# Staggered SBUF places for the operands of the matrix products

## The chip, the core and the metric

The kernel runs on one core of a Trainium2 chip. The metric is device time in microseconds of one execution. Two runs of the kernel before took 2041.06 and 2042.29 us, median 2041.67.

## What is computed

Two transformer blocks, one after the other, on a sequence of 512 tokens of width 1024, in float32. Cut to the products, which are nearly all of the work:

```python
# first block
x = x + 0.5 * swiglu(rmsnorm(x, ffn1_norm), ffn1_wgu, ffn1_wdown)   # d_ff 2816
z = rmsnorm(x, mix_norm) @ w_in                                      # q, k, v, conv, gates
a = sliding_window_attention(q, k, v, sinks) @ attn_proj
c = silu(layernorm(causal_depthwise_conv(u, dw_w, dw_b))) @ conv_proj
x = x + (sigmoid(ga) * a + sigmoid(gb) * c) @ w_out
x = x + 0.5 * swiglu(rmsnorm(x, ffn2_norm), ffn2_wgu, ffn2_wdown)
x = x + sigmoid(rmsnorm(x, ple_gate_norm) @ ple_gate_w) * rmsnorm(p @ ple_proj, ple_norm)
# second block
h = h + concat(pool_mixer(...), deltanet_mixer(...)) @ w_out_2       # from rmsnorm(h) @ w_in_2
h = h + memory_cross_attention(rmsnorm(h), rmsnorm(mem), w_xq, w_xk, w_xv, w_xo)
h = h + relu(rmsnorm(h) @ w_up) ** 2 @ w_down                        # d_ff 4096
return rmsnorm(h, final_norm_g)
```

## The kernel before

Activations lie transposed: a tile of 128 partitions, eight chunks (one for each 128 of the 1024 channels) and 512 tokens in a chunk. Weights come as *units*: one unit is the block of 128 output channels over all input channels, a tile of 128 x 1024 (eight parts of 128 columns; fewer in some units). `unit_plan` lists all 357 of them in the order of use.

Each product is made in three steps to keep float32 accuracy. A float32 operand is split into a high part, written as float32r by the scalar engine (a rounding copy), and a low part, the difference, written by the vector engine. `w_split` does this for a unit's weights: the staged tile `wst` becomes `wh` (L188, ACT) and `wl` (L189, DVE). `split` does it for activations (`xh` and `xl`, `hh` and `hl`, and others). `mm3` then issues, for one part k, three matmuls into the same PSUM tile: wh x xh (L227), wh x xl (L228), wl x xh (L229). The weights' 128 columns are the stationary operand, loaded anew by TensorE for every matmul; the 512 (or 256) tokens of an activation chunk are the moving operand. A unit is eight such triples, and then its PSUM tile is evacuated.

The order on PE is the program's; a scheduler places the other engines' work. Weight transfers run four units ahead (`AHEAD_DMA`), splits two (`AHEAD_SPLIT`); `wst` has two buffers, `wh` and `wl` three each.

Places in SBUF, as the built program has them (byte offsets in a partition). The eight-chunk tiles all come from `big`: five buffers of 16,384 bytes at 27328 + 16384 n, chunk k at 2048 k in them. `wh` has its three buffers at 135872 + 4096 n, `wl` at 148160 + 4096 n, part k at 512 k in them. Each of these starts 704 bytes past a multiple of 2048. In the cross attention of the second block, the products of `xhead` (L1360) read the stationary operand from `xv` (at 176832, again 704 past a multiple of 2048, its pieces at multiples of 512) and the moving one from `pth` and `ptl` (201536 and 205632, both 832 past a multiple of 2048).

In `dn_blocks` (the delta rule's 16 x 16 triangular blocks) a vector operation multiplies into a small temporary of 16 x 15 with a buffer of its own, tag `t16`; another temporary there, `g16`, is 16 x 16.

Of the kernel before, what the change touches and what calls it, by code (L numbers as in the profile page):

```python
# [9 lines left out]
F32 = mybir.dt.float32  # L10
F32R = mybir.dt.float32r
# [4 lines left out]
P = 128  # L16
S = 512
D = 1024
ND = D // P
# [87 lines left out]
class Kern:  # L107
# [18 lines left out]
        return f"{s}_{self.n}"  # L126

    def big(self, s, dt=F32):
        return self.pb.tile([P, 8, S], dt, tag="b16", name=self.nm(s), bufs=5)

    def c5(self, s, bufs=10):
        return self.pm.tile([P, 542], F32, tag="c5", name=self.nm(s), bufs=bufs)
# [43 lines left out]
    def w_split(self, i, parts=1):  # L176
        if i >= len(self.plan) or i in self.split_:
            return
        self.w_dma(i)
        nb = self.plan[i][2]  # L180
        st = self.staged[i]
        h = self.pw.tile([P, nb * P], F32R, tag="wh", name=self.nm("wh"), bufs=3)
        l = self.pw.tile([P, nb * P], F32R, tag="wl", name=self.nm("wl"), bufs=3)
        self.split_[i] = (h, l)
        n = nb * P // parts
        for p in range(parts):
            c = slice(p * n, p * n + n)
            r = self.nc.scalar.copy(h[:, c], st[:, c])  # L188
            self.nc.vector.tensor_tensor(out=l[:, c], in0=st[:, c], in1=h[:, c].bitcast(F32), op=ALU.subtract)  # L189
        return r  # L190
# [774 lines left out]
    def dn_blocks(self):  # L965

        nc = self.nc
        v = nc.vector.tensor_tensor  # L970
        u16 = self.pm.tile([P, 16, 16], F32, tag="u16", name="u16")
        ex = lambda t: t.rearrange("p (a c) -> p a c", c=1).to_broadcast([P, 16, 16])
        d16 = self.lcol("d16").rearrange("p (a c) -> p a c", a=1).to_broadcast([P, 16, 16])
        nc.gpsimd.tensor_copy(u16[:], d16)
        sel = []
        for q in range(4):
            sel.append(self.pm.tile([P, 4, P], F32R, tag="A1", name=self.nm("sel"), bufs=4))
            nc.gpsimd.tensor_tensor(
                out=sel[q][:], in0=self.lcol("bd16").rearrange("p (a c) -> p a c", a=1).to_broadcast([P, 4, P]),
                in1=self.bc(self.lcol("d16")[:, 4 * q:4 * q + 4], 4), op=ALU.mult)  # L980
        while self.fronts < 4:
            yield
        g16 = self.pm.tile([P, 16, 16], F32, tag="g16", name="g16")
        v(out=g16[:], in0=ex(self.g_br[:]), in1=d16, op=ALU.mult)
        yield
        ps = self.pd()
        nc.tensor.matmul(ps[:, :256], self.lcol("bd16"), g16[:].rearrange("p a c -> p (a c)"), start=True, stop=True)
        v(out=g16[:], in0=ps[:, :256].rearrange("p (a c) -> p a c", c=16), in1=self.ld[:], op=ALU.mult)
        self.split(self.ldh[:], self.ldl[:], g16[:])
        yield  # L990
        for js in ((0, 1), (2, 3), (4, 5, 6), (7, 8, 9, 10, 11), (12, 13, 14)):
            ps, o = self.pd(), 0
            reps = []
            for j in js:
                w = 16 - j - j % 2
                r = ps[:, o:o + 16 * w].rearrange("p (a c) -> p a c", c=w)
                sj = sel[j // 4][:, j % 4, :]
                nc.tensor.matmul(r, sj, self.ldh[:, :, 16 - w:], start=True, stop=False)
                nc.tensor.matmul(r, sj, self.ldl[:, :, 16 - w:], start=False, stop=True)
                reps.append((j, 15 - j, r[:, :, w - 15 + j:]))  # L1000
                o += 16 * w
            for j, w, r in reps:
                t = self.pm.tile([P, 16, 15], F32, tag="t16", name=self.nm("t16"))
                v(out=t[:, :, :w], in0=r, in1=u16[:, :, j:j + 1].to_broadcast([P, 16, w]), op=ALU.mult)
                v(out=u16[:, :, j + 1:], in0=u16[:, :, j + 1:], in1=t[:, :, :w], op=ALU.add)
            if js[0] == 4:
                yield
        self.u16 = u16
# [637 lines left out]
```

## Time and profile before

| | |
|---|---|
| runs, median | 2041.67 us (2041.06 to 2042.29) |
| the profiled execution | 2041.87 us, span 2040.1 us |
| PE busy | 97% of the span, 9324 matmuls |
| DVE, ACT, POOL busy | 59%, 43%, 13% |
| TensorE clock granted, mean | 0.990 of full speed |
| HBM traffic | 98 GB/s over the span |

The span runs from the first to the last instruction of the profiled execution. Busy time of PE counts overlapping, pipelined matmuls, so it does not tell how fast they follow each other; for that one reads the starts in the timeline. A matmul's record is longer (0.39 us with 512 columns) than the distance to the next start, as matmuls overlap. [...]

### The profile page before, as it was taken

The page shows a single profiled execution, that of the slowest core. Times are in us where ns is not written, and L with a number is a line of the kernel's source. Part 1 is how long each engine was busy: PE and PEld are TensorE (multiplying, and loading weights), DVE is VectorE, ACT ScalarE, POOL GpSimd, SP SyncE. Part 2 cuts the span into 40 slices and gives each one's busy share as a digit, 9 for nine tenths or more (in the row PEclk, how much of TensorE's full clock was granted, in tenths as well). Part 3 has the DMA queues.
Part 4 walks back from the last instruction along what each step waited for, and adds up shares of the span by engine and source line. Part 5 has one row for each costly group of instructions (what it writes and reads, how often), then busy time and mean ns, then how long its engine had stood idle before and what let it go on. Part 6 is the DMA issues. An engine that isn't in the chain of part 4 may idle for free. (4 is left out here: it accounts for less than half of the span.)

```text
span 2040.1 us, 24509 instructions
## 1 busy us (share of the span) xinstructions
PE 1982.6 (97%) x9324; PEld 1649.1 (81%) x9324; DVE 1209.1 (59%) x1909; ACT 875.9 (43%) x1437; POOL 272.7 (13%) x263
## 2 busy tenths in 40 slices
PE   8999999999998999999999999997999999999997
PEld 6888888788787888888888877876989888888886
DVE  6434435799889865543443577666576655344344
ACT  5213223565878543431322364364364444233233
POOL 0000000196224300000000003257000000000001
PEclk9999999999899999999999999998999999999999
DMA  5232233323122134223223234212044422232322
GB/s 182 93 104 93 96 100 103 127 89 101 62 75 65 58 129 158 95 93 100 97 93 103 83 94 136 91 57 83 22 154 131 135 83 93 98 99 93 102 94 73
DMA packets 65669, 200.92 MB, mean 98 GB/s; under 512 B 7312, under 2 KB 11536, under 8 KB 65424
## 3 DMA queue, kind: packets, MB, share of 16 engines
q1 hardware_dynamic: 64864, 198.83, 29.8%
q8 instruction: 74, 1.21, 0.3%
q10 hardware_dynamic: 688, 0.53, 0.1%
q14 instruction: 43, 0.35, 0.1%
HBM read 188.58 MB, written 10.49 MB: 98 GB/s over the span
## 5 line engine op out<-in xcount | busy, mean ns | idle before, releaser
L188 ACT CAST wh<-wst 128x1024 fp32r<-128x1024 f32 (+3 forms) x357 | 353.9, 993 | 894.9 <-PE mm L228 641.0
L227 PE MATMUL mm<-xh,wh 128*128 128x512 f32 x1272 | 502.2, 395 | 2.6 <-ACT xh L291 1.5
L229 PE MATMUL mm<-xh,wl 128*128 128x512 f32 x1272 | 495.7, 390 | 0.7 <-DVE wl L189 0.5
L228 PE MATMUL mm<-xl,wh 128*128 128x512 f32 x1272 | 495.5, 390 | 0.3 <-DVE xl L292 0.3
L189 DVE TENSOR_TENSOR wl<-wst,wh 128x1024 fp32r<-128x1024 f32 (+3 forms) x357 | 421.5, 1182 | 76.8 <-ACT wh L188 76.4
L227 PEld LDWEIGHTS mm<-xh,wh 128*128 128x128 f32 x1272 | 239.0, 188 | 55.1 <-issue 2.7
L228 PEld LDWEIGHTS mm<-xl,wh 128*128 128x128 f32 x1272 | 239.2, 188 | 52.6 <-issue 3.1
L229 PEld LDWEIGHTS mm<-xh,wl 128*128 128x128 f32 x1272 | 239.1, 188 | 51.4 <-DVE wl L189 1.5
L228 PE MATMUL mm<-hl,wh 128*128 128x512 f32 (+1 forms) x616 | 238.2, 387 | 0.2
L227 PE MATMUL mm<-hh,wh 128*128 128x512 f32 (+1 forms) x616 | 238.3, 387 | 0.0
L229 PE MATMUL mm<-hh,wl 128*128 128x512 f32 (+1 forms) x616 | 237.9, 386 | 0.0
L372 DVE SCALAR_TENSOR_TENSOR x<-mm,x 128x512 f32<-128x512 f32 x111 | 76.7, 691 | 249.3 <-PE mm L229 249.3
L652 POOL TENSOR_TENSOR y<-y,cv 128x512 f32<-128x512 f32 x90 | 131.7, 1463 | 126.0 <-ACT cv L651 109.3
L228 PEld LDWEIGHTS mm<-hl,wh 128*128 128x128 f32 x616 | 115.7, 188 | 24.4 <-DVE hl L289 1.0
L227 PEld LDWEIGHTS mm<-hh,wh 128*128 128x128 f32 x616 | 115.7, 188 | 23.5
L229 PEld LDWEIGHTS mm<-hh,wl 128*128 128x128 f32 x616 | 115.7, 188 | 23.2
L227 PE MATMUL mm<-xnh,wh 128*128 128x512 f32 x304 | 120.8, 397 | 0.7 <-DVE z L390 0.7
L228 PE MATMUL mm<-xnl,wh 128*128 128x512 f32 x304 | 119.6, 393 | 0.0
L229 PE MATMUL mm<-xnh,wl 128*128 128x512 f32 x304 | 119.5, 393 | 0.0
L439 DVE TENSOR_TENSOR t<-mm,R 128x512 f32<-128x512 f32 x43 | 29.7, 692 | 138.4 <-PE mm L229 138.3
L660 DVE SCALAR_TENSOR_TENSOR cacc<-u,vec,cacc 128x512 f32<-128x512 f32 x145 | 108.9, 751 | 2.8
L433 DVE TENSOR_TENSOR t<-mm,R 128x512 f32<-128x512 f32 x43 | 29.7, 692 | 94.1 <-PE mm L229 94.0
(421 smaller groups left out, 2800.5 us busy)
## 6 DMA issues: line engine op xcount, KB each, us to landing
wst<-ffn_wgu SPq DMA_DIRECT2D x86, 512.0 KB, 3.4
wst<-w_in SPq DMA_DIRECT2D x63, 512.0 KB, 3.5
wst<-ffn_wdown SPq DMA_DIRECT2D x32, 512.0 KB, 3.5
wst<-w_up SPq DMA_DIRECT2D x32, 512.0 KB, 3.4
wst<-w_down SPq DMA_DIRECT2D x32, 512.0 KB, 3.4
wst<-ffn_wdown SPq DMA_DIRECT2D x16, 384.0 KB, 3.0
xd<-x SPq DMA_DIRECT2D x24, 256.0 KB, 2.3
x<-xd SPq DMA_DIRECT2D x24, 256.0 KB, 5.0
```

Source lines behind the costliest of these rows:

```text
L188: r = self.nc.scalar.copy(h[:, c], st[:, c])
L189: self.nc.vector.tensor_tensor(out=l[:, c], in0=st[:, c], in1=h[:, c].bitcast(F32), op=ALU.subtract)
L227: self.last_mm = mm(ps, h, xh, start=first, stop=False)
L228: mm(ps, h, xl, start=False, stop=False)
L229: mm(ps, l, xh, start=False, stop=last)
L372: self.nc.vector.scalar_tensor_tensor(out=x, in0=ps[:], scalar=scale, in1=x, op0=ALU.mult, op1=ALU.add)
L433: nc.vector.tensor_tensor(out=t[:], in0=ps[:], in1=R[:], op=ALU.mult)
L439: nc.vector.tensor_tensor(out=t[:], in0=ps[:], in1=R[:], op=ALU.mult)
L652: eng.tensor_tensor(out=y, in0=y, in1=t[:], op=ALU.add)
L660: yield eng.scalar_tensor_tensor(out=y if j == 29 else acc, in0=u[:, j:j + S], scalar=w(j), in1=acc, op0=ALU.mult, op1=ALU.add)
```

## The change

Three edits, all on where tiles lie.

- `big` allocates eight chunks of 516 instead of 512 columns and hands out the first 512 of each. So chunk k starts 2064 k bytes into the tile, 16 k bytes further than before, and the five buffers lie 16,512 bytes apart.
- `w_split` always allocates 1036 columns for `wh` and `wl` (1024 and 12 spare ones) and places the unit's parts 4 (i mod 4) columns into the buffer, i being the unit's number in the plan: 0, 16, 32 or 48 bytes. The weight buffers lie 4,160 bytes apart, at 136512 + 4160 n and 148992 + 4160 n.
- The temporary of `dn_blocks` becomes 16 x 16 and shares the tag, hence the buffer, of `g16`, which frees the room that the others take.

Tiles that are allocated behind these move along; `xv` is now at 177856, `pth` at 202560. On every engine's queue the same instructions stand in the same order with the same waits as before; the one row that reads otherwise is a vector multiplication of `dn_blocks` whose output is now 16 x 15 with gaps and was 240 columns in a row.

```diff
     def big(self, s, dt=F32):
-        return self.pb.tile([P, 8, S], dt, tag="b16", name=self.nm(s), bufs=5)
+
+        return self.pb.tile([P, 8, S + 4], dt, tag="b16", name=self.nm(s), bufs=5)[:, :, :S]
...
         st = self.staged[i]
-        h = self.pw.tile([P, nb * P], F32R, tag="wh", name=self.nm("wh"), bufs=3)
-        l = self.pw.tile([P, nb * P], F32R, tag="wl", name=self.nm("wl"), bufs=3)
+        o = 4 * (i % 4)
+        h, l = (self.pw.tile([P, ND * P + 12], F32R, tag=t, name=self.nm(t), bufs=3)[:, o:o + nb * P]
+                for t in ("wh", "wl"))
         self.split_[i] = (h, l)
...
-                t = self.pm.tile([P, 16, 15], F32, tag="t16", name=self.nm("t16"))
+                t = self.pm.tile([P, 16, 16], F32, tag="g16", name=self.nm("t16"))
                 v(out=t[:, :, :w], in0=r, in1=u16[:, :, j:j + 1].to_broadcast([P, 16, w]), op=ALU.mult)
```

## Rows read from the trace of the kernel before

**Rows 1.** The page's first part: busy us, share of the span, instructions.
```profile
PE 1982.6 (97%) x9324; PEld 1649.1 (81%) x9324; DVE 1209.1 (59%) x1909; ACT 875.9 (43%) x1437; POOL 272.7 (13%) x263
```

**Rows 2.** Table by stage: length, busy us and instructions by engine, clock, DMA share, GB/s.
```profile
core 0: us, PE busy (x) PEld busy (x) DVE busy (x) ACT busy (x) POOL busy (x), PEclk, DMA share, GB/s
0.00:510.00 510.00, 501.80 (x2206) 412.55 (x2206) 308.09 (x407) 209.30 (x288) 91.12 (x61) 1.00 0.33 109
510.00:663.00 153.00, 139.64 (x728) 119.93 (x729) 136.53 (x353) 122.13 (x282) 47.02 (x35) 0.96 0.21 67
663.00:1173.00 510.00, 509.39 (x2250) 420.54 (x2249) 270.16 (x343) 179.63 (x238) 19.11 (x13) 1.00 0.31 101
1173.00:1428.00 255.00, 233.32 (x1068) 185.82 (x1066) 176.02 (x314) 130.53 (x246) 104.29 (x140) 0.97 0.29 92
1428.00:2018.00 590.00, 588.38 (x3013) 501.38 (x3013) 307.24 (x477) 228.22 (x378) 4.38 (x8) 1.00 0.30 98
```

**Rows 3.** Timeline of PE in the first feed-forward block: start, length, line, operation.
```profile
299.94 0.39 PE L227 MATMUL mm<-xh,wh 128*128 128x512 f32 x1
...
305.83 0.39 PE L229 MATMUL mm<-xh,wl 128*128 128x512 f32 x1
```

**Rows 4.** Timeline of PE, products with 256 moving columns (the memory's keys).
```profile
1537.33 0.28 PE L228 MATMUL mm<-mem,wh 128*128 128x256 f32 x1
...
1538.89 0.28 PE L229 MATMUL mm<-mem,wl 128*128 128x256 f32 x1
```

**Rows 5.** Groups by line and form: count | busy us, mean ns | idle us before.
```profile
L227 PE MATMUL mm<-xh,wh 128*128 128x512 f32 x1272 | 502.2, 395 | 2.6 <-ACT xh L291 1.5 <-ACT wh L188 1.1
...
L227 PE MATMUL mm<-hh,wh 128*128 128x512 f32 x600 | 233.4, 389 | 0.0
...
L227 PE MATMUL mm<-xnh,wh 128*128 128x512 f32 x304 | 120.8, 397 | 0.7 <-DVE z L390 0.7
...
L227 PE MATMUL mm<-ch,wh 128*128 128x512 f32 x64 | 24.9, 389 | 0.0
```

**Rows 6.** Table by stage, a stretch of the attention with lowered clock.
```profile
514.50:517.20 2.70, 2.70 (x15) 2.70 (x14) 2.47 (x9) 2.33 (x6) 0.00 (x0) 0.50 0.08 15
```

**Rows 7.** Timeline of PE in that stretch, attention's scores, 256 moving columns.
```profile
514.95 0.41 PE L228 MATMUL pd<-kpl,qh 128*128 128x256 f32 x1
...
517.09 0.41 PE L229 MATMUL pd<-kph,ql 128*128 128x256 f32 x1
```

**Rows 8.** Timeline of PE behind products of another shape, at two places.
```profile
377.57 0.39 PE L228 MATMUL mm<-xl,wh 128*128 128x512 f32 x1
...
379.88 0.39 PE L229 MATMUL mm<-xh,wl 128*128 128x512 f32 x1
...
496.53 0.40 PE L227 MATMUL mm<-xnh,wh 128*128 128x512 f32 x1
...
498.62 0.39 PE L227 MATMUL mm<-xnh,wh 128*128 128x512 f32 x1
...
501.79 0.39 PE L229 MATMUL mm<-xnh,wl 128*128 128x512 f32 x1
```

**Rows 9.** Timeline of PE, first head of the cross attention.
```profile
1563.50 0.40 PE L227 MATMUL pd<-pth,xv 128*128 128x512 f32 x1
...
1566.29 0.28 PE L227 MATMUL mm<-mem,wh 128*128 128x256 f32 x1
```

**Rows 10.** Table by stage, the same products in the second and third head.
```profile
1592.91:1595.70 2.79, 2.79 (x13) 2.25 (x12) 2.38 (x3) 2.16 (x3) 0.00 (x0) 1.00 0.00 0
1619.46:1622.25 2.79, 2.79 (x14) 2.27 (x13) 2.29 (x4) 1.64 (x2) 0.00 (x0) 1.00 0.89 299
```

**Rows 11.** Table by stage for line L227 alone: PE and PEld, busy us and count.
```profile
510.00:663.00 153.00, 62.43 (x164) 32.91 (x165) 0.96 0.21 67
...
1173.00:1428.00 255.00, 109.99 (x270) 50.68 (x269) 0.97 0.29 92
```

**Rows 12.** The page's fifth part: weight splits on ACT, idle before them and its end.
```profile
L188 ACT CAST wh<-wst 128x1024 fp32r<-128x1024 f32 (+3 forms) x357 | 353.9, 993 | 894.9 <-PE mm L228 641.0
```

**Rows 13.** Waits of PE: us in total, times, longest.
```profile
PE pd L227 <- ACT xh L291: 7.0, 2, 5.1
```

## Prediction

> **What bounds the kernel now.** I read the page's busy times first: TensorE is busy 97% of the span, no other engine over 59% [rows 1]. A busy PE is not a PE at its peak, so the next view is the table by stage [rows 2]. In three stretches, together 1,610 of 2,040 us, PE's idle time is 8.2 + 0.6 + 1.6 us, while PE runs 2,206 + 2,250 + 3,013 products. Nothing can be late in these stretches but PE itself; their time is the number of products times the distance from one start to the next. The other two long stretches (510 to 663, 1173 to 1428) have 13.4 and 21.7 us of PE idle time, and a longer product there is partly paid out of waiting.
>
> So the number to watch is the distance between starts. In the steady run of the first feed-forward block, 26 of them take 305.83 - 299.94 = 5.89 us, 226.5 ns each [rows 3]. With 256 moving columns, 13 of them take 1.56 us, 120 ns each [rows 4]. The 256 columns more cost 106.5 ns, one column per cycle of the 2.4 GHz clock (256/2.4 = 106.7); what is left, 120 - 106.7 = 13.3 ns, does not grow with the columns. It is 6% of a 512-column product, and there are 7,632 of those: the seven groups of L227 in [rows 5] (four of them alike, one shown) have 1272 + 600 + 304 + 4 x 64 = 2,432, each thrice (L227, L228, L229), which makes 7,296, and groups of 16 or 32 the rest.
>
> Is this 13.3 ns a fixed price of an instruction? Two rows say no. Where the granted clock is 0.50 of full speed, the 1.2 GHz level [rows 6], ten products of 256 columns take 2.14 us from start to start, 214 ns each, against 256/1.2 = 213.3 [rows 7]: read at half the pace, nearly nothing is left over. And at full clock the distance depends on circumstances. After other shapes have run on PE, the products go unevenly for a while: nine take 498.62 - 496.53 = 2.09 us (232.2 ns each), ten take 379.88 - 377.57 = 2.31 us (231.0), and then the run falls back by itself: the next 14 behind the nine take 501.79 - 498.62 = 3.17 us, 226.4 each [rows 8]. It looks as if two streams that are read together, the moving operand and the next weights, step on each other's accesses, by an amount that their relative timing decides, and as if the stream settles into a cheap relation.
>
> **What the change does.** By the order of the built programs it moves no instruction and no wait on any engine; only one vector operation's shape is written 16x15 instead of 240. What changes are places. Before, each moving chunk and each weight chunk of these products starts 704 bytes past a multiple of 512 x 4, or that plus a multiple of 512: the distance between the two streams is 0 modulo 512 in all of them. Afterwards it takes many values: the five big buffers start 128 bytes apart modulo 2048, their chunk k another 16 k, the weight buffers 64 bytes apart, and the unit's number adds 0, 16, 32 or 48.
>
> The trace of before has one place where that distance is not 0: the products of cross attention that read pth and ptl (832 past a multiple of 2048) against xv (704), 128 bytes off. They are 12 in a row in each of four heads. In the first these take 1566.29 - 1563.50 = 2.79 us [rows 9], and stretches laid from the first start to the start behind the twelfth are 2.79 us long in the next two as well [rows 10]: 232.5 ns each. They do not settle to 226.5 in those 12, where other unsettled runs did within ten. Other causes I can see are poor: the DMA share is 0.00 in the second head and 0.89 in the third, with the same time, and PE is busy throughout in both [rows 10]. It is a sample of one distance, but the only one.
>
> The sum:
> - Products that settle at 226.5 now will, I take it, run at about 231 ns, since the relation changes with each chunk (every third product) and the nine or ten that settling took before are never left in peace. Bounds: 0 if places do not matter, 232.5 - 226.5 = 6 ns if all of them go like pth, and -12.6 if the conflict vanished and of the 13.3 only the half-clock row's 214 - 213.3 = 0.7 were left [rows 4, 7]. I take +4.5, the lower of the two unsettled rows (231.0 - 226.5 = 4.5, and 232.2 - 226.5 = 5.7) [rows 8], since these are the same operands with the settled relation lost, and some chunks may find a cheap relation at once.
> - How many pay: the two stretches with waits hold (164 + 270) x 3 = 1,302 of the three-product kind [rows 11]; I count half of these and all of the other 7,632 - 1,302 = 6,330, together 6,980, so about 7,000. 7,000 x 4.5 ns = **+32 us**.
> - Writing the shifted tiles: 357 weight splits of 993 ns on ACT, and DVE's part behind each. ACT waits 641 us in all before its part for PE to free a buffer [rows 12], so it is early by far; at a tenth longer each the product still does not wait. 0; without that cover 357 x 0.1 = +36 us, which the idle time excludes.
> - Transfers into and out of x, now 16 k bytes on per chunk. Of these the first load is in the open: PE waits 7.0 us at the start for xh [rows 13], which is made from x. I take 0, since the rows of 2 KB stay whole; if the loads took twice as long, those 7 us would come once more. The spills and reloads lie under full PE stretches; the last outputs are as open as the first loads, and I have no separate price for them.
> - The temporary of 15 columns now shares g16's buffer. Its 15 products on DVE start behind matmuls that read what was made from g16, so the buffer is free by then: 0.
>
> 2041.9 (the profiled execution's own time; the median of the runs is 2041.7) + 32 = **2074 us**.
>
> [...]
>
> **The rivals.**
> - *Places don't matter* (0.15). For it: 226.5 holds in the big stages though the moving tile lies in five different buffers and the weights in three. Against: all of these are alike modulo 512, and pth, which is not, differs. Time: 2034 to 2050.
> - *The conflict goes away* (0.22), the faster side. The two streams start at the same line today in every product. If it is just this that costs the 13.3 ns, four staggered places of 16 bytes would spare three products in four: 0.75 x 12.6 x 7,000 = 66 us, hence 1976; if a third of the stall goes, 4.2 x 7,000 = 29 us, 2013. For it: at half the pace the stall is gone [rows 6, 7], so something can be won. Against: pth's offset of 128 bytes makes the distance longer, not shorter, and no run of 512-column products that I read is under 226. It decides once the average distance is below 221 ns.
> - *All go like pth or worse* (0.23). 6 ns x 7,000 = 42 us: 2084; at 240 ns, 95 us and 2136, for which no run of several products speaks.
> - *Unsettled, as summed* (0.40): +1.2 to +5.9 ns, 2050 to 2083.
>
> **How the numbers follow.** The likeliest case gives 2074, its own range is 2050 to 2083. Leaving out the deeper half of the relieved cases and the far end of the pth-like ones gives 2005 to 2094. Two per cent, about what a measurement of this kernel tells from no change, is 41 us: faster than 2001 needs over half the possible relief, 0.12; slower than 2083 is the pth-like case, 0.23; the rest, 0.65, lies between, with more of it above 2042 than below.
>
> **What would show it.** In the changed profile the order and the waits should be as they are, PE's idle time in the three full stretches too; only the distance between starts should move. Right: a timeline of 299 to 306 with uneven distances of 0.22 to 0.24 us, mean near 0.231, and about 221 to 222 products in a stretch of 51 us that holds 226 now. Wrong: 226 again (places don't matter), 230 or more (relief), or an unchanged distance with new idle time before PE, which would be a transfer or a split. The step that is weakest is the one from pth's four heads to all products.

## The result, and the profile after

| | before | after |
|---|---|---|
| runs, median | 2041.67 us (2041.06 to 2042.29) | 2066.99 us (2065.66 to 2068.32) |
| the profiled execution | 2041.87 us, span 2040.1 us | 2068.32 us, span 2066.5 us |
| ratio of the times, 95% interval | | 1.0121 (1.0105 to 1.0137) |
| mean distance of the starts, 512-column weight products in undisturbed units | 226.7 ns | 231.7 ns |

The changed kernel is 25.3 us slower, 1.2%, against 32 us foretold. It is inside the 2% band, and on the side that the likeliest case named. (The mean distances here and below are worked out from the starts in the trace: over all units of 24 or more such products in which no two neighbouring starts lie 300 ns or more apart.) One slip in the part on the kernel: the plan holds 351 units, not 357; the 357 are the weight splits, since the first two units are split in four parts each. One of the ten executions of the kernel with the temporary alone, below, took 7381.93 us for a reason that no trace shows, and is left out of its ratio.

The first part of the page of the changed kernel, to be read against [rows 1]:

```profile
PE 2014.1 (97%) x9324; PEld 1647.6 (80%) x9324; DVE 1210.0 (59%) x1909; ACT 874.8 (42%) x1437; POOL 274.2 (13%) x263
```

Only PE has become longer, by 31.5 us of busy time with the same 9,324 matmuls. The other engines are within 1.5 us of what they were. The table by stage of the changed kernel (length, busy us and instructions by engine, clock, DMA share, GB/s), with a piece of 51 us from the first feed-forward block:

```profile
0.00:510.00 510.00, 502.81 (x2157) 405.19 (x2158) 299.47 (x384) 202.57 (x273) 90.09 (x61) 1.00 0.33 107
663.00:1173.00 510.00, 508.54 (x2210) 412.05 (x2209) 265.76 (x339) 176.28 (x239) 24.78 (x17) 1.00 0.30 99
102.00:153.00 51.00, 51.00 (x222) 41.33 (x221) 19.32 (x21) 10.61 (x11) 0.00 (x0) 1.00 0.29 93
```

And the same 51 us of the kernel before:

```profile
102.00:153.00 51.00, 51.00 (x226) 42.24 (x226) 17.33 (x19) 10.02 (x10) 0.00 (x0) 1.00 0.30 104
```

PE is as full as in [rows 2] and the granted clock is 1.00 in both, yet 222 products start where 226 did. In these two of the three full stretches 49 and 40 products fewer fit in. Nothing new is waited for: span minus busy time of PE is 52.4 us where it was 57.5. Each product stands further from the next. The timeline of PE (start, length, line, operation) at the place of [rows 3]; L229, L230 and L231 are what L227, L228 and L229 were:

```profile
299.00 0.40 PE L229 MATMUL mm<-xh,wh 128*128 128x512 f32 x1
299.23 0.39 PE L230 MATMUL mm<-xl,wh 128*128 128x512 f32 x1
299.45 0.40 PE L231 MATMUL mm<-xh,wl 128*128 128x512 f32 x1
299.69 0.39 PE L229 MATMUL mm<-xh,wh 128*128 128x512 f32 x1
...
305.95 0.40 PE L229 MATMUL mm<-xh,wh 128*128 128x512 f32 x1
```

The first distances are 0.23, 0.22 and 0.24 us: uneven. Thirty of them take 305.95 - 299.00 = 6.95 us, 231.7 ns each, against 226.5 in [rows 3]. That is the whole change; the rest of this text asks what decides the distance, and why 7,584 weight products of 512 columns at 5.0 ns more (38 us) made only 26.

### The profile page after: what moved, and what is told of

Its sections match the earlier page's. It is cut to its first block, busy times and chain, and to the rows that moved or that the text cites. A ratio compares the mean times of both kernels' runs of the same rounds, so it can differ in the third digit from the quotient of the medians.

```text
span 2066.5 us, 24509 instructions
## 1 busy us (share of the span) xinstructions
PE 2014.1 (97%) x9324; PEld 1647.6 (80%) x9324; DVE 1210.0 (59%) x1909; ACT 874.8 (42%) x1437; POOL 274.2 (13%) x263
## 5 line engine op out<-in xcount | busy, mean ns | idle before, releaser
L229 PE MATMUL mm<-xh,wh 128*128 128x512 f32 x1272 | 506.8, 398 | 1.6 <-ACT wh L190 1.2
L231 PE MATMUL mm<-xh,wl 128*128 128x512 f32 x1272 | 501.7, 394 | 0.7 <-DVE wl L191 0.7
L230 PE MATMUL mm<-xl,wh 128*128 128x512 f32 x1272 | 500.7, 394 | 0.3 <-DVE xl L294 0.3
L229 PEld LDWEIGHTS mm<-xh,wh 128*128 128x128 f32 x1272 | 239.1, 188 | 59.4 <-issue 2.4
L230 PEld LDWEIGHTS mm<-xl,wh 128*128 128x128 f32 x1272 | 239.3, 188 | 58.1 <-issue 2.9
L231 PEld LDWEIGHTS mm<-xh,wl 128*128 128x128 f32 x1272 | 238.9, 188 | 56.9 <-DVE wl L191 1.5
L231 PE MATMUL mm<-hh,wl 128*128 128x512 f32 (+1 forms) x616 | 241.1, 391 | 0.0
L229 PE MATMUL mm<-hh,wh 128*128 128x512 f32 (+1 forms) x616 | 241.0, 391 | 0.0
L230 PE MATMUL mm<-hl,wh 128*128 128x512 f32 (+1 forms) x616 | 240.7, 391 | 0.0
L230 PEld LDWEIGHTS mm<-hl,wh 128*128 128x128 f32 x616 | 115.9, 188 | 27.3 <-DVE hl L291 0.9
L229 PEld LDWEIGHTS mm<-hh,wh 128*128 128x128 f32 x616 | 115.7, 188 | 26.2
L231 PEld LDWEIGHTS mm<-hh,wl 128*128 128x128 f32 x616 | 115.6, 188 | 26.1
L229 PE MATMUL mm<-xnh,wh 128*128 128x512 f32 x304 | 121.7, 400 | 0.6 <-DVE z L392 0.6
L230 PE MATMUL mm<-xnl,wh 128*128 128x512 f32 x304 | 120.3, 396 | 0.0
L231 PE MATMUL mm<-xnh,wl 128*128 128x512 f32 x304 | 120.2, 395 | 0.0
```

The costliest lines, as they stand in the source:

```text
L229: self.last_mm = mm(ps, h, xh, start=first, stop=False)
L230: mm(ps, h, xl, start=False, stop=False)
L231: mm(ps, l, xh, start=False, stop=last)
```

## The experiments

Two theories went into the runs. **Settling (S)**: the two streams, the moving operand and the weights that are loaded meanwhile, fall into a cheap relation whenever their distance in SBUF stays the same from one chunk to the next, and the change costs because each chunk has another distance. **Distance (D)**: the distance itself decides, some are cheap and some are dear however long they last. "Distance" is, throughout, where the next product's weights start minus where the running product's moving chunk starts, in bytes, modulo 256 unless said otherwise; it comes from the places in the built programs. The next product's weights are taken because, in the trace of the kernel before, the load of them starts 3 ns behind the start of the running product and takes 188 ns (medians over the weight products). The third possibility, that places don't matter, was left from the rivals.

The kernel before was timed beside each run; its median was 2042.13 us in all three groups of runs.

**The weights alone.** Only the weights' places (and the temporary); the chunks stay where they were. A unit's two weight parts lie 148992 - 136512 = 12,480 bytes apart, 192 modulo 256, so a unit has two distances, 64 bytes apart, which come back in the same order in each of its triples. The expectation overlooked this; it has the distance change only from unit to unit.

```diff
-        h = self.pw.tile([P, nb * P], F32R, tag="wh", name=self.nm("wh"), bufs=3)
-        l = self.pw.tile([P, nb * P], F32R, tag="wl", name=self.nm("wl"), bufs=3)
+        o = 4 * (i % 4)
+        h, l = (self.pw.tile([P, ND * P + 12], F32R, tag=t, name=self.nm(t), bufs=3)[:, o:o + nb * P]
+                for t in ("wh", "wl"))
```

> The weights' half of the change alone: weight buffers 64 bytes further apart, unit i another 16 (i mod 4) bytes; the eight-chunk tiles as before. Theory S (settling): the spacing settles whenever the distance between moving operand and weights stays the same from one chunk to the next; here it changes only from unit to unit, so about 10 of a unit's 24 products are unsettled: 10/24 x 4.5 ns x 7,000 = +13 us, 2055 us. Theory D (distance): each distance has its own price and 0 modulo 512 is a cheap one; nearly all units leave 0, so the spacing is about 231 ns throughout, 2065 to 2075 us. Theory C (the chunks' shift alone is the cause): 2042 us.

Measured: 2067.55 us (2066.31 to 2068.59), ratio 1.0128 (1.0111 to 1.0145), mean distance of starts 231.6 ns. By D it was to be about 231 ns, and each pair of distances has a price of its own, from 230.0 to 235.6 ns over the last twelve distances of a unit. No pair settles at 226.7, though each chunk repeats the one before: S as put falls. Units with one distance only, which decide it, come with the rulers below.

**The chunks alone.**

```diff
-        return self.pb.tile([P, 8, S], dt, tag="b16", name=self.nm(s), bufs=5)
+        return self.pb.tile([P, 8, S + 4], dt, tag="b16", name=self.nm(s), bufs=5)[:, :, :S]
```

> The other half alone: chunk k of the eight-chunk tiles 16 k bytes on (buffers 128 bytes apart modulo 2048), weight buffers as before. S: the distance changes at every third product, nothing settles, 2067 us as with the whole change. D: distances spread over many values, about the same 2060 to 2075 us. If the weights' shift were the cause alone: 2042 us.

Measured: 2071.18 us, ratio 1.0145 (1.013 to 1.016), mean distance of starts 232.0 ns. Each half of the change alone costs as much as both together or more: their costs don't add. Each alone already takes the operands off their common place, which is the likely reason.

**The temporary alone.** Only the last edit of the diff, `t16` into the buffer of `g16`.

> The third edit alone: the 16 x 15 temporary of the delta rule becomes 16 x 16 and shares its buffer with g16; no operand of the big products moves. All theories: 2042 us, within 2 us of before. Above 2045 us it would have a share of its own in the change's +25 us.

Measured: 2041.53 us, ratio 0.9997 (0.9987 to 1.0007). It has no effect, as the sum had it.

**A ruler in steps of 16 bytes.** Both weight parts of unit i lie 16 (i mod 32) bytes into their buffers, chunks as before. All products of a unit have one distance, and the program walks through 32 of them eleven times over. To make room, `t2` has five buffers instead of six.

```diff
+        o = 4 * (i % 32)
+        h, l = (self.pw.tile([P, ND * P + 128], F32R, tag=t, name=self.nm(t), bufs=3)[:, o:o + nb * P]
+                for t in ("wh", "wl"))
```

> A ruler: the eight-chunk tiles as before, the unit's weights 16 (i mod 32) bytes into buffers that lie 4608 bytes apart, so that the distance is 16 (i mod 32) modulo 512, the same for all products of a unit and for both weight parts; one temporary buffer of six is given up for the room. S: every unit settles within about 10 products and its second half runs at 226.7 ns whatever the offset. D: the second half of a unit has its own spacing by offset: 226.7 at 0, about 232 to 233 at 128 (the cross attention's distance before), others between 224 and 238, the same for all units of one offset.

Measured: 2066.3 us. The timeline of PE in this kernel, the first products of six units, 24 products apart each:

```profile
277.20 0.39 PE L228 MATMUL mm<-xh,wh 128*128 128x512 f32 x1
...
282.64 0.39 PE L228 MATMUL mm<-xh,wh 128*128 128x512 f32 x1
...
288.09 0.39 PE L228 MATMUL mm<-xh,wh 128*128 128x512 f32 x1
...
293.68 0.40 PE L228 MATMUL mm<-xh,wh 128*128 128x512 f32 x1
...
321.64 0.40 PE L228 MATMUL mm<-xh,wh 128*128 128x512 f32 x1
...
327.24 0.39 PE L228 MATMUL mm<-xh,wh 128*128 128x512 f32 x1
```

The unit at 277.20 has distance 0: 5.44 us, 226.7 ns each. The next has 16: 5.45 us, 227.1, the same within the records' digits. The next has 32: 5.59 us, 232.9. The one at 321.64 has 128: 5.60 us, 233.3. Over the whole kernel, the mean of a unit's last twelve distances of starts, by distance in bytes (13 to 19 units each; distances 256 apart agree and stand together):

| distance | ns |
|---|---|
| 0, 16, 240 | 226.7 |
| 192, 176 | 229.4, 230.0 |
| 80 | 232.1 |
| 32, 48, 64, 112, 128, 144, 160, 208, 224 | 233.3 |
| 96 | 234.3 |

Not one of them is below the kernel before. The cheap ones lie around 0 and repeat after 256 bytes. This holds for 512 columns. With 256 columns (the memory's keys and values) the common place is among the dear ones: their mean, over neighbouring starts, is 119.6 ns in the kernel before and 119.0 with all at 128 bytes (the padded kernel below), and 118.1 in the changed kernel.

**The same ruler in steps of 4 bytes**, at 0 to 124 bytes and at 128 to 252 bytes (`o = i % 32`, and `o = 32 + i % 32`).

> The same ruler in steps of 4 bytes, 0 to 124. S: 226.7 ns in the second half of every unit. D: the price changes with the offset; if it goes by 16-byte lines, four neighbouring offsets have the same spacing, or the offsets that are no multiple of 16 are dearer by themselves, for 32 + 1 lines in place of 32 per weight part.

> The ruler of 4-byte steps for offsets 128 to 252 (0 to 124 are measured), one temporary buffer of six given up. D: 240 at 226.7 ns, 176 and 192 near 229.5 to 230, the rest 230 to 235. What would matter for a faster kernel: an offset whose products settle under 226.7 ns. Expected: none, since none of 0 to 124 does.

Measured: 2071.54 and 2072.67 us. In the lower half 0 and 120 give 226.7 ns; 12, 44, 60, 100 and 108 give 230.0; 8 and 24 give 230.8 and 231.1; the rest 231.7 to 235.0. In the upper half 132, 156, 228 and 252 give 226.7, nine units in ten at 204 and eight in ten at 144 do as well, and the other distances lie between 228.3 and 238.1. The expectation missed 240, which runs at 228.3 in all nine units, and had none of the cheap ones. So a place that isn't a multiple of 16 is not dear by that, some such places are as cheap as 0, and again none is cheaper.

These two runs also keep a piece of S. At distance 16 the first ruler gave 226.7 in all 14 units, the lower of these 233.3 in nine units of ten. The tenth, at 610 us, begins with distances of 236, 235, 233 and 232 ns and then runs at 226.7 to its end. At 144 the first ruler gave 233.3, the upper of these 226.7 in eight units of ten and 233.3 in those at 609 and 1554 us. So at some distances more than one steady pattern exists. What chooses is not shown; what ran just before is likely, since these three odd units come right behind products of other shapes, and the rulers differ in the distance of the unit before (0 against 12 for 16).

**A shift of the weights by 128 bytes, and by 256.** Nothing is staggered: an unused tile is allocated ahead of the weights, 128 bytes in one kernel and 256 in the other. What is allocated behind moves along; the heads' operands keep their distance of 128.

```diff
+        self.pad = self.pw.tile([P, 32], F32, tag="pad", name="pad")     # 64 instead of 32 in the other kernel
```

> The kernel before with one unused tile of 128 bytes a partition ahead of the weight buffers: nothing staggered, every distance between moving operand and weights is 128 modulo 256 instead of 0. Theory D (distance, from the ruler: 233.5 ns at 128): (233.4 - 226.7) x 7,000 = +47 us, 2089 us, slower than the whole change. Theory S (any constant distance settles): 2042 us.

> The same with an unused tile of 256 bytes. D with its period of 256 bytes: 226.7 ns, 2042 us, as before. If a shift as such costs something, or the weights' own place modulo 512 or 2048 counts: above 2050 us.

Measured: 2073.29 us (2073.15 to 2074.03), ratio 1.0153 (1.0138 to 1.0168), and 2042.33 us, ratio 1.0001 (0.9991 to 1.001). PE's timeline with 128 bytes:

```profile
299.09 0.39 PE L228 MATMUL mm<-xh,wh 128*128 128x512 f32 x1
...
306.05 0.39 PE L228 MATMUL mm<-xh,wh 128*128 128x512 f32 x1
```

and with 256:

```profile
299.11 0.39 PE L228 MATMUL mm<-xh,wh 128*128 128x512 f32 x1
...
305.91 0.39 PE L228 MATMUL mm<-xh,wh 128*128 128x512 f32 x1
```

Thirty distances each: 6.96 us, 232.0 ns, and 6.80 us, 226.7 ns. One line that allocates a tile nobody reads costs 31 us, and twice that tile costs nothing. This is the cleanest of the runs: places matter, by 256 bytes, and nothing else of the change is needed. The size was missed: 2089 was expected of the first, from about 7,000 products at 6.7 ns; 31.2 us at the measured 232.4 - 226.7 = 5.7 ns are 5,500 of them.

**The cross attention's heads moved to distance 0.** An unused tile of 128 bytes behind `xv`, so that `pth` and `ptl` come to lie like all other operands.

> The kernel before with an unused tile of 128 bytes behind xv, so that pth and ptl lie 0 modulo 256 from xv in the cross attention; nothing else is staggered. Theory D: the twelve products of each head settle to 226.7 ns, 2.72 us in place of 2.79; the time within 1 us of before (48 x 6 ns = 0.3 us). If the heads' spacing before had another cause than the places, it stays at 232.5 to 233.3 ns.

Measured: 2042.62 us. The timeline of PE, the first head's first product and the start behind its twelfth:

```profile
1564.50 0.39 PE L227 MATMUL pd<-pth,xv 128*128 128x512 f32 x1
...
1567.22 0.28 PE L227 MATMUL mm<-mem,wh 128*128 128x256 f32 x1
```

2.72 us for the twelve, 226.7 ns each; they took 2.79 at 128 bytes [rows 9]. In the changed kernel, where they are still 128 bytes off, they take 2.80:

```profile
1581.89 0.40 PE L229 MATMUL pd<-pth,xv 128*128 128x512 f32 x1
...
1584.69 0.28 PE L229 MATMUL mm<-mem,wh 128*128 128x256 f32 x1
```

The inference from these heads, which the prediction called its weakest step, was right in its cause.

**Both operands staggered alike.** Weight part k and chunk k both lie 16 k bytes further, so that the distance is 0 within a triple and 16 from a triple's last product to the next part.

```diff
+        t = self.pb.tile([P, 8 * S + 64], dt, tag="b16", name=self.nm(s), bufs=5)
+        return t[:, :8 * (S + 4)].rearrange("p (c s) -> p c s", s=S + 4)[:, :, :S]
...
+        h, l = (self.pw.tile([P, ND * P + 64], F32R, tag=t, name=self.nm(t), bufs=3)[:, :nb * (P + 4)]
+                .rearrange("p (k c) -> p k c", c=P + 4)[:, :, :P] for t in ("wh", "wl"))
```

> Both operands staggered alike: chunk k of the eight-chunk tiles 16 k bytes on as in the change, part k of the weights 16 k bytes on too, buffers at multiples of 256 from each other; the distance stays 0 (16 where the next part's weights are loaded beside the third product of a chunk); one temporary buffer of six given up for the room. D, distance alone decides: 226.7 ns, 2042 to 2047 us. If the places of the one or the other operand by themselves, or the shift from chunk to chunk, cost the time: 231 to 233 ns, 2065 to 2090 us.

Measured: 2063.18 us, ratio 1.0104 (1.0087 to 1.0121). The timeline of PE, thirty distances:

```profile
298.88 0.39 PE L229 MATMUL mm<-xh,wh 128*128 128x512 f32 x1
...
305.80 0.39 PE L229 MATMUL mm<-xh,wh 128*128 128x512 f32 x1
```

6.92 us, 230.7 ns each; 230.1 over the last twelve distances of a unit. D expected 226.7 here, since 0 and 16 are both cheap on the first ruler. It missed: distance alone isn't all, a step of 16 bytes in both streams at every third product keeps costing 3.4 ns. Why stays open. One thing more can be read here. From the fourth chunk on the distances of starts repeat every two chunks, 32 bytes: 232, 228 and 231 ns with both operands at 240, 16 or 48 modulo 256, and 228, 229 and 232 at 0 or 32. So over these places, in steps of 32 bytes, it doesn't matter where both lie together, only where they lie against each other.

**Only `wl` moved**, by 16 (i mod 16) bytes, so that one product in three has another distance than 0.

```diff
+        o = 4 * (i % 16)
+        l = self.pw.tile([P, ND * P + 64], F32R, tag="wl", name=self.nm("wl"), bufs=3)[:, o:o + nb * P]
```

> The ruler for the low parts alone: wl of unit i 16 (i mod 16) bytes into its buffer, wh and all else at distance 0. In a triple L227, L228, L229 the weights loaded beside the running product are wh, wl, wh. If the price is that of the load beside the running product, L228's spacing changes with the offset and the two others' by what phase it leaves; if it is that of a product's own weights, L229's. Offsets 0 and 16 (and 240) should stay at 226.7 by theory D; whether some mixed arrangement runs under 226.7 is open.

Measured: 2063.43 us. With wl at 0, 16, 240 and, nearly always, 144 the mean of the last twelve distances stays at 226.7 to 227.0 ns; at the others it is 230.7 to 233.3, and all three products of the triple are disturbed (at 32: 232.6, 239.0 and 228.4 ns, from the first to the third). One dear distance in three costs most of what three cost, and mixing is not what costs in the run above: here 0 and 16 in turn are cheap.

## Why the prediction was right, and where two errors met

**That order and waits stay and only the distance moves: right.** 222 products in 51 us were expected to be 221 to 222; the mean was expected near 231 ns and is 231.7.

**The price: too low by a tenth.** The sum took 4.5 ns, the lower of the two unsettled rows of [rows 8]; measured are 231.7 - 226.7 = 5.0, between 4.5 and the 5.7 of the other row. The reason given, settled relations that are lost at each chunk, is half of the story: by the runs with one distance per unit, most distances have no cheap relation to settle into (on the ruler of 16-byte steps 13 of 16 stay at 229.4 to 234.3 ns over the last twelve distances of a unit).

**The count: too high.** The sum had 7,000 paying products: all of 6,330 outside the two stretches with waits, half of the 1,302 in them. (The 1,302 are L227's products of all widths, and 56 x 3 = 168 of them are the attention's with 256 columns, which the 7,632 leave out; 1,134 is right, 7,065 payers, and little changes.) 26.4 us of span at 5.0 ns are 5,280. The starts of all weight products, which stand in the same order in both traces, show where the rest went (times of the kernel before; what each stretch grew by):

| stretch, us | 512-column weight products | at 5.0 ns, us | grew by, us |
|---|---|---|---|
| 0 to 475 | 2,029 | 10.1 | 9.9 |
| 475 to 510 | 131 | 0.7 | -1.7 |
| 510 to 663 | 324 | 1.6 | -1.0 |
| 663 to 1173 | 2,203 | 11.0 | 10.2 |
| 1173 to 1428 | 809 | 4.0 | 0.8 |
| 1428 to 1632 | 401 | 2.0 | 0.1 |
| 1632 to 2022 | 1,687 | 8.4 | 8.1 |

Where PE alone sets the pace, everyone pays: 28.2 us for 29.5, and the rest is idle time of PE, which fell from 3.4 to 2.2 us in these three. In the other four stretches 1,665 products should have brought 8.3 us and brought -1.9. Half of the products with waits nearby was too many: none of them paid in sum. Added up from the first product of each stretch as the table does, PE's idle time in these four fell from 36.9 to 32.9 us, and the full-speed time that a lowered clock took from its busy time from 12.1 to 8.8: together about 7.3 of the 10.2 us. So three things gave time back, of which the prediction had allowed for the first alone, with its half.

First, waits. PE's work before a wait takes longer, the other engine's doesn't, so PE waits less. The largest is in the attention, in PE's timeline of the kernel before (in brackets the idle time ahead and what ended it):

```profile
511.71 0.38 PE L605 MATMUL pd<-cst,s 128*128 128x128 f32 x1 [2.17 <-ACT s L591]
```

The same product in the changed kernel:

```profile
520.29 0.33 PE L607 MATMUL pd<-cst,s 128*128 128x128 f32 x1 [0.41 <-ACT s L593]
```

1.76 us of the wait are gone, and the lowered clock behind it is shorter by half (0.57 on average over 511 to 519 us before, 0.79 over 519 to 527 after). It is why the stretch of 475 to 510 became shorter: it is counted from the start of its first weight product to that of the first one behind it, and this wait lies ahead of the latter.

Second, the clock. Waits and clock are seen together there and, more clearly, early in the second block. The timeline of PE before:

```profile
1256.72 0.39 PE L229 MATMUL mm<-xh,wl 128*128 128x512 f32 x1
1258.58 0.49 PE L227 MATMUL mm<-xh,wh 128*128 128x512 f32 x1 [1.48 <-ACT xh L291]
1259.37 0.80 PE L228 MATMUL mm<-xl,wh 128*128 128x512 f32 x1 [0.29 <-DVE xl L292]
1259.96 0.63 PE L229 MATMUL mm<-xh,wl 128*128 128x512 f32 x1
1260.39 1.91 PE L351 MATMUL sm<-ss,cst 128*128 128x512 f32 x2
1261.31 1.42 PE L227 MATMUL mm<-xh,wh 128*128 128x512 f32 x1
1262.53 0.52 PE L228 MATMUL mm<-xl,wh 128*128 128x512 f32 x1
1262.88 0.40 PE L229 MATMUL mm<-xh,wl 128*128 128x512 f32 x1
```

and the same instructions in the changed kernel:

```profile
1275.44 0.39 PE L231 MATMUL mm<-xh,wl 128*128 128x512 f32 x1
1276.31 0.49 PE L229 MATMUL mm<-xh,wh 128*128 128x512 f32 x1 [0.48 <-ACT xh L293]
1277.10 0.49 PE L230 MATMUL mm<-xl,wh 128*128 128x512 f32 x1 [0.29 <-DVE xl L294]
1277.43 0.40 PE L231 MATMUL mm<-xh,wl 128*128 128x512 f32 x1
1277.66 1.02 PE L353 MATMUL sm<-ss,cst 128*128 128x512 f32 x2
1278.12 0.79 PE L229 MATMUL mm<-xh,wh 128*128 128x512 f32 x1
1278.75 0.39 PE L230 MATMUL mm<-xl,wh 128*128 128x512 f32 x1
1278.98 0.39 PE L231 MATMUL mm<-xh,wl 128*128 128x512 f32 x1
```

1262.88 - 1256.72 = 6.16 us have become 1278.98 - 1275.44 = 3.54. The wait for xh is 1.0 us shorter. The other 1.6 us are products that ran at half pace, as the table by stage says of the kernel before and of the changed one:

```profile
1260.00:1262.00 2.00, 2.00 (x5) 0.97 (x3) 0.68 (x1) 1.04 (x1) 0.51 (x1) 0.50 0.28 103
```

```profile
1278.00:1280.00 2.00, 2.00 (x9) 1.42 (x8) 1.25 (x2) 1.84 (x3) 0.96 (x1) 1.00 0.21 78
```

Before, PE had been idle for 1.48 and 0.29 us, and the granted clock then stood at 0.50; after idle times of 0.48 and 0.29 us it stayed at 1.00. The same happened at 550 us, where the kernel before has the clock at 0.50 and the changed one does not. There the wait ahead hardly differs (2.25 us before, 2.14 after), so less waiting does not explain that one. Over the whole span the lowered clock took away 20.0 us of full-speed time before and 15.8 after, though part of that lies where PE waits anyway. The two drops near 550 and 1260 stand in all four traces with undisturbed distances (the kernel before, 256 bytes of padding, the temporary, the heads); of the nine disturbed ones none has the first, and only the one with both operands staggered alike has the second, while the chunks alone and `wl` alone have one near 1220 us that the kernel before lacks.

Third, the stretch from 1428 to 1632 was not at 226.7 before. There the products alternate with other shapes, their mean distance was 228.1 and is 231.4 now, 3.3 ns instead of 5.0, or 1.3 us instead of 2.0. The 256-column products among them take a little less than the 120 ns of [rows 4], 1.5 ns less on average over 384 of them, which gives back 0.6 us: thirteen take 1.54 us, 118.5 each, in the timeline of the changed kernel:

```profile
1555.27 0.28 PE L229 MATMUL mm<-mem,wh 128*128 128x256 f32 x1
...
1556.81 0.28 PE L230 MATMUL mm<-mem,wh 128*128 128x256 f32 x1
```

What is left, about 1 us in the stretch of 1173 to 1428, is not explained. Price and count erred in opposite directions, 5.0 x 5,280 = 26 against 4.5 x 7,000 = 32, so a part of the closeness is luck; with the right price alone the forecast would have been 2077 us, 10 too high.

**The terms at 0: right.** The weight splits in the page's fifth part, against [rows 12], and the waits of PE for the first load, against [rows 13]:

```profile
L190 ACT CAST wh<-wst 128x1024 fp32r<-128x1024 f32 (+3 forms) x357 | 352.9, 989 | 927.0 <-PE mm L230 691.0
```

```profile
PE pd L229 <- ACT xh L293: 6.6, 2, 5.3
```

989 ns instead of 993 for a split, and ACT waits longer for PE than before, 691 instead of 641 us. The first wait is 6.6 instead of 7.0 us. Spills took 2.1 us instead of 2.3 from issue to landing, reloads 5.3 instead of 5.0; all in cover.

**The rivals.** That places don't matter is refuted by the two padding kernels: both would then be at 2042, and with 128 bytes it is 2073.29. The 232.4 ns there against 226.7 with 256 bytes, at a granted clock of 1.00 in both (102 to 153 us) and with nothing but the length of an unused tile between them, say that places do cost. That the conflict goes away is refuted by the four rulers for products of 512 columns: no unit's mean is under 226.6 ns. What a product takes beyond its columns, 13.3 ns in the prediction, is still there at the cheapest distance, and what it is stays open. No trace gives the clock in GHz, only as a share of full speed: 2.4 is what the 106.5 ns for 256 columns [rows 3, 4] come to in columns per ns, and by these alone the 13.3 are 226.5 - 2 x 106.5 = 13.5, and the 213.3 for the row at half clock are 213.0. Nor does a trace show the lines that this rival and the expectation for 4-byte steps speak of; what the programs show is a distance of 0 modulo 512, and the rulers show a price by distance. That all go like pth was nearer than its chance said in price (the chunks alone make 232.0, 128 bytes of padding 232.4), but its 2084 was built on the same count and would have come to 2073.

What is not settled: what the hardware does at a dear distance. Sums and one period were measured, no mechanism; and the kernel with both operands staggered alike shows that a table by distance doesn't foretell a mixture. No run moves both operands by one same constant. That their distance counts and not each one's own place rests on this: moving either alone costs (chunks alone, padding), and moving the heads' operand to its partner's place takes the cost away.

## What to carry to other kernels

When TensorE is full and runs products with a weight load each, look at the distance of starts as a quantity of its own, and compute from the allocation where moving operand and weights lie against each other: here 0 modulo 256 bytes was as good as any found for 512 columns (226.7 ns; for 256 columns it was not, 119.6 against 118.1 in the changed kernel), and an allocation 128 bytes long ahead of the weights cost 1.5%. After any edit that moves tiles, also one that moves no instruction, compare thirty starts in a steady stretch before and after. And count as payers only the products of stretches in which PE never waits; in the others the longer products were free in sum here (8.3 us were due, -1.9 came), since waits and lowered clock gave most of the time back, about 7.3 us.

## What the runs showed of the hardware

- A float32r product of 512 columns with a weight load takes 226.7 ns from start to start at a granted clock of 1.00 at the best places and 233.3 at most others. Sustained means bunch at 226.7, 230.0 and 233.3, with others between and a few up to 238.1.
- With 256 columns it takes 119.6 ns with all operands at the common place and 118.1 in the changed kernel: the common place, the cheapest found for 512 columns (226.7), is not the cheapest for 256.
- The pattern repeats with 256 bytes (on the ruler of 16-byte steps, and with padding: 232.4 ns at 128 bytes, 226.7 at 256), but does not go by blocks of 16 or 32 bytes: 120, 132, 156, 228 and 252 are as cheap as 0, while 4 bytes beside them (124, 128, 152, 232, 248) cost 4 to 7 ns.
- At some distances (16, 144) there are two steady patterns, 226.7 and 233.3; what chooses between them was not shown, and that it is what ran before a unit is an inference from three units.
- Less waiting and a higher granted clock can pay for longer products: 1.6 of the 2.6 us saved at one place (6.16 to 3.54 us) came with a clock that was not lowered there, 1.00 instead of 0.50.
